# Layer 0 of a two-layer trunk: smaller triangular inverses, one shared tile, and a new order of the steps

## The chip, the cores and the metric

The kernel runs on one core of a Trainium2 chip. The metric is the device time of one launch in microseconds. The kernel before was timed in three runs: median 1544.08 us, from 1541.60 to 1544.83.

## The reference

The program is a two-layer encoder trunk over 1024 tokens of width 1024, in float32, with a conditioning vector that scales, shifts and gates each layer. Layer 0 feeds one input projection into two kinds of bidirectional heads; layer 1 (a 31-tap convolution and dilated attention) is not touched by the change but for the place of its tiles. What matters here is layer 0, cut to its core:

```python
# even layer: four mLSTM heads (dk 64, dv 128) and four gated DeltaNet heads (128, 128)
mq, mk, mv, mo, mg, dqkv, dg, z = split(h @ w_in)
# mLSTM, per chunk, state C:  num = w*(q @ C) + (exp(d - m) * (q k^T)) @ v ;  C = wold*C + kw^T v
out_a = sigmoid(mo) * head_rms(mlstm(forward) + mlstm(backward))
# DeltaNet: qkv = silu(conv5(dqkv)), q and k normalised per head
a    = strict_tril(beta * (k k^T) * gam)
u, w = solve(a + I, beta*v), solve(a + I, beta*exp(gc)*k)     # the triangular inverse
v_new = u - w @ S ;  o = (q*exp(gc)) @ S + (q k^T * gam) @ v_new
S     = exp(gl)*S + (k*exp(gl - gc))^T v_new
out_b = head_rms(gdn(forward) + gdn(backward))
mix   = concat(out_a, out_b) * silu(z) ;  y = mix @ w_out ;  x = x + gate * y
```

The recurrences run over chunks, forward and backward, so a step of either kind needs the state of the step before it in its direction.

## The kernel before, in words

Tokens are cut into eight chunks of 128 (`NCH`). Activations lie transposed, features on partitions. A projection of 128 output columns (`in0`, through `project` and `prod`) splits weights and activations into a high and a low part and sums three products: 2 halves of tokens x 8 blocks of features x 3 = 48 matmuls of 512 columns. `wsplit` loads the weights on SP's queue, ScalarE makes the high part, GpSimd the low part (line 241). Output tiles (`y`, in `out_tile`) are 48 matmuls each as well.

Instructions are written in program order and a scheduler orders each engine's queue by it, with program order as priority; each engine then runs its queue in order and waits on semaphores. Nearly all DMAs of layer 0 go out from SP's one queue, also in order. Weight columns for the modulation (`modulation`, lines 428 to 432) are loaded and summed a piece at a time between projections.

Layer 0 in program order: the first key projections and gates; `dn_scales`; eight `dn_system` calls (per chunk: `KK` = k k^T, decay masks built by ScalarE and GpSimd, products on VectorE at line 637, a transpose `NT`, both stored to DRAM); then a list of steps: DeltaNet queries and values (`dn_q`, `dn_v`: a projection, a five-tap convolution on VectorE at lines 373 to 391, turns by TensorE), mLSTM queries, keys and values (`m_q`, `m_k`, `m_v`), all eight mLSTM steps at once (`mlstm`), `dn_inverse`, and the first gates; then the eight `dn_step` calls, the other gates (`gate_chunk`, `gate_pair`: z and mo projections), and the output tiles (`out0`).

`dn_inverse` holds 128 triangular blocks of 64x64 (2 directions, 2 halves, 8 chunks, 4 heads), one on each partition, as `NL`, and eliminates column by column on VectorE: per column a product into `iv` (line 663) and an addition (line 666), cut in halves where the rectangle passes 512 elements. It then stores the blocks to DRAM (`xl_d`) as they are and transposed. `dn_step` loads its piece as `Y`, joins the two blocks of a chunk with two small products `T` through `aux`, and then computes `kS`, `Yr`, `KQ`, `qS`, `dS` and `o`, for direction 0 (`d=0`) and then direction 1.

PSUM: two banks for projections, and a pool of banks `t`, `A`, `B`, `C` (1, 2, 2, 1) for the rest. SBUF: pools on the right side that are opened and closed as the layer goes on.

## Time and profile before

| what | value |
|---|---|
| median of three runs | 1544.08 us |
| the profiled execution's own time | 1542.68 us |
| its span in the trace | 1540.9 us |
| mean granted clock of TensorE | 0.928 |
| TensorE, VectorE, ScalarE, GpSimd busy | 1338.6, 979.4, 635.4, 605.3 us |
| layer 0, layer 1 | 0 to some 884 us, 884 to 1541 us |

Sums are made against the profiled execution; the 1.8 us between its time and its span are start and end, and it is 1.4 us below the median. In the rows below, PE is TensorE, PEld its weight loads, DVE VectorE, ACT ScalarE, POOL GpSimd, SP the engine that issues DMAs. A row of windows has the stretch, its length, busy time and number of instructions of PE, PEld, DVE, ACT and POOL, then the granted clock as a share of 2.4 GHz, the share of the DMA engines and GB/s. A row of a group has the line, engine, operation, output and inputs, shapes and count, then busy time and mean duration in ns, then idle time before it; matmuls overlap, so a mean is more than the distance from one to the next. A row of one line (`x106: a/b/c`) has the shortest, median and longest duration in ns, then the first and last start.

### The profile page before, as it was taken

To read this page: it belongs to the slowest core of one execution; us is meant where nothing else is said; L and a number is where in the kernel's file an instruction comes from. 1 tells how busy PE (TensorE), PEld (TensorE's weight loads), DVE (VectorE), ACT (ScalarE), POOL (GpSimd) and SP (SyncE) were. 2 spreads that over 40 slices of the span, in tenths; PEclk is the share of its full clock that TensorE was granted. 3 is DMA by queue.
4 is the path that set the end of the run, shared out by engine and by line. 5 is a ranking of instruction groups with operands and counts; after the bars stand their busy time and mean duration, and the time that the engine had idled before them with its cause. 6 is when DMAs were issued, how large, how long until landed. Compare 5 with 4: busy or idle time off the path is not lost.

```text
span 1540.9 us, 20550 instructions
## 1 busy us (share of the span) xinstructions
PE 1338.6 (87%) x7195; PEld 1059.1 (69%) x7195; DVE 979.4 (64%) x1712; ACT 635.4 (41%) x1481; POOL 605.3 (39%) x433
## 2 busy tenths in 40 slices
PE   3978767887877889889999979778999999999998
PEld 2767655666665667778877857556777777777776
DVE  6789346999889442345854427999984445345544
ACT  5354456433444513433453323335335633425322
POOL 3562325563464332110243117998514215122210
PEclk9999987998888999979999999989999899998999
DMA  9333669444654886454736261001123115244332
GB/s 312 94 91 78 130 143 235 129 125 135 184 165 133 276 267 203 117 155 145 224 118 205 83 135 49 28 28 42 42 87 111 48 56 189 73 123 157 120 113 107
DMA packets 235658, 202.50 MB, mean 131 GB/s; under 512 B 38591, under 2 KB 198867, under 8 KB 235427
## 3 DMA queue, kind: packets, MB, share of 16 engines
q1 hardware_dynamic: 214755, 190.70, 42.9%
q10 hardware_dynamic: 20800, 10.49, 2.4%
q8 instruction: 57, 0.93, 0.3%
q14 instruction: 46, 0.38, 0.1%
HBM read 146.87 MB, written 57.93 MB: 133 GB/s over the span
## 4 chain that ended last, share of the span: by engine, by line
PE 35%; DVE 11%; DMA 4%; issue 2%; ACT 2%; POOL 0%; SPq 0%; ACTq 0%; POOLq 0%; DVEq 0%
PE y L121 9%; DVE u L1220 8%; PE z L121 6%; PE sc L121 3%; PE av L121 3%; PE ob L121 2%; PE pT L136 2%; PE aq L121 2%; PE ak L121 2%; DMA z_d<-nb_d 1%; PE gb L121 1%; PE vps L136 1%; DMA g<-mix_d 1%; ACT junk L1040 1%; PE dS L121 0%
## 5 line engine op out<-in xcount | busy, mean ns | idle before, releaser
L241 POOL TENSOR_TENSOR wlo<-wraw,whi 128x1024 fp32r<-128x1024 f32 x60 | 158.2, 2637 | 238.5 <-ACT whi L240 224.8
L1220 DVE SCALAR_TENSOR_TENSOR u<-xp,cw,u 128x1009 f32<-128x1009 f32 (+14 forms) x90 | 174.6, 1941 | 2.1
L1210 POOL TENSOR_TENSOR u<-u,cv 128x512 f32<-128x512 f32 (+15 forms) x60 | 120.5, 2010 | 17.3 <-ACT cv L1209 13.8
L432 POOL TENSOR_TENSOR macc<-macc,ada 128x512 f32<-128x512 f32 x56 | 89.6, 1599 | 76.9 <-ACT ada L430 64.1
L121 PE MATMUL z<-hhi,whi 128*128 128x512 f32 x256 | 106.8, 417 | 1.9 <-ACT mo L719 1.9
L121 PE MATMUL z<-hlo,whi 128*128 128x512 f32 x256 | 105.5, 412 | 0.0
L121 PE MATMUL z<-hhi,wlo 128*128 128x512 f32 x256 | 105.4, 412 | 0.0
L121 PE MATMUL y<-wohi,mhi 128*128 128x512 f32 x240 | 96.4, 403 | 1.4 <-ACT mhi L1010 1.4
L121 PE MATMUL y<-wohi,mlo 128*128 128x512 f32 x240 | 95.4, 399 | 0.6 <-DVE mlo L1011 0.5
L121 PE MATMUL y<-wolo,mhi 128*128 128x512 f32 x240 | 95.9, 399 | 0.0
L240 ACT CAST whi<-wraw 128x1024 fp32r<-128x1024 f32 x60 | 62.6, 1043 | 72.4 <-PE gb L121 15.6
L666 DVE TENSOR_TENSOR NL<-NL,iv 128x440 f32<-128x440 f32 (+40 forms) x106 | 92.1, 897 | 0.5
L663 DVE TENSOR_TENSOR iv<-NL 128x440 f32<-128x440 f32 (+40 forms) x106 | 87.5, 858 | 1.4
L591 POOL TENSOR_SCALAR_AFFINE_SELECT E<-E 128x512 f32<-128x512 f32 x32 | 22.7, 709 | 149.0 <-DMA E<-gc_d 57.6
L430 ACT ACTIVATE ada<-ada,cs 128x512 f32<-128x512 f32 x56 | 40.4, 725 | 80.7 <-DMA ada<-in_ada_w_dram 79.6
L1209 ACT ACTIVATE cv<-xp,cw 128x512 f32<-128x512 f32 (+15 forms) x60 | 42.4, 718 | 55.5 <-POOL u L1210 55.2
L1372 DVE COPY PT<-pT 128x512 f32<-128x512 f32 x48 | 32.4, 688 | 48.2 <-PE pT L136 48.1
L1349 ACT ACTIVATE pt<-pt,o 128x256 f32<-128x256 f32 (+1 forms) x64 | 31.4, 491 | 75.6 <-DVE o L1345 73.2
L121 PEld LDWEIGHTS z<-hhi,whi 128*128 128x128 f32 x256 | 49.7, 194 | 14.9 <-ACT mo L719 2.3
L121 PEld LDWEIGHTS z<-hlo,whi 128*128 128x128 f32 x256 | 49.8, 195 | 11.7 <-issue 1.1
L121 PEld LDWEIGHTS z<-hhi,wlo 128*128 128x128 f32 x256 | 49.8, 195 | 11.6 <-issue 1.0
L1345 DVE CUSTOM_DVE_ANT_0 pt<-sc,bias 128x256 f32<-128x256 f32 (+1 forms) x64 | 25.8, 403 | 48.8 <-PE sc L121 28.8
(449 smaller groups left out, 3718.5 us busy)
## 6 DMA issues: line engine op xcount, KB each, us to landing
wraw<-in_ev_w_in_dram SPq DMA_DIRECT2D x32, 512.0 KB
ada<-in_ada_w_dram SPq DMA_DIRECT2D x64, 256.0 KB
wraw<-in_od_w_in_dram ACTq DMA_DIRECT2D x20, 512.0 KB
x<-in_x_dram SPq DMA_DIRECT2D x16, 512.0 KB
ada<-in_ada_w_dram SPq DMA_DIRECT2D x16, 512.0 KB
od_d<-o SPq DMA_DIRECT2D x64, 66.0 KB
n<-od_d SPq DMA_DIRECT2D x4, 1056.0 KB
E<-nmu_d SPq DMA_DIRECT2D x16, 256.0 KB
```

What stands on the lines that cost most here:

```text
L121: return nc.tensor.matmul(o, lhsT=l, rhs=r, start=s, stop=e, skip_group_check=shared).ins
L136: nc.tensor.transpose(o, i, ident[:k, :k])
L240: nc.scalar.copy(out=hi, in_=raw)
L241: nc.gpsimd.tensor_tensor(out=lo, in0=raw, in1=f(hi), op=ALU.subtract)
L430: nc.scalar.mul(out=t_ if k else acc, in_=t_, mul=cs[:, k:k + 1])
L432: nc.gpsimd.tensor_tensor(out=acc, in0=acc, in1=t_, op=ALU.add)
L663: nc.vector.tensor_tensor(out=t_, in0=NL[:, a_:b_, k:k + 1].to_broadcast([P, b_ - a_, m]), in1=NL[:, k:k + 1, k + 1:64].to_broadcast([P, b ...
L666: nc.vector.tensor_tensor(out=NL[:, a_:b_, k + 1:64], in0=NL[:, a_:b_, k + 1:64], in1=t_, op=ALU.add)
L1209: nc.scalar.mul(out=t_, in_=xp[:, lo + d:hi + d], mul=w_)
L1210: nc.gpsimd.tensor_tensor(out=y[:, lo:hi], in0=y[:, lo:hi], in1=t_, op=ALU.add)
L1220: nc.vector.scalar_tensor_tensor(out=y[:, lo:hi], in0=xp[:, lo + d:hi + d], scalar=w_, in1=y[:, lo:hi], op0=ALU.mult, op1=ALU.add)
L1372: nc.vector.tensor_copy(out=PT, in_=tb)
```

## The change

Five things are changed together.

1. **One tile.** The right-side pools are gone; one tile `U` of 128 x 8448 floats is there for the whole kernel, and `sl` and `ring` cut slices and rotating slices out of it. The six early PSUM banks become the fixed pool `psb` from the start. Some tags get other banks: turns use only bank `t`, T and KQ too; kS, Yr and dS are on `A`, qS and o on `C`; the mLSTM products on `B`. Both directions of `dn_step` draw E from one ring of two, `aux` has one buffer.
2. **The inverse.** VectorE eliminates only the 32x32 diagonal blocks (30 columns, 30 products and 30 additions). The off-diagonal block of each 64x64 block is computed on TensorE as a product of three, in four rounds: `first_product` spreads Z over a block diagonal on VectorE (ZD), iG multiplies it by AT; GD spreads that, iV multiplies by B, iT transposes the result. Z, AT and B are read back from `xl_d` by 12 DMAs, and the results are written back to it by 8.
3. **The order.** The systems and the inverse come after two value projections and the first DeltaNet head; the mLSTM and DeltaNet steps come one by one between the gate projections and, at the end, the output tiles.
4. **mLSTM operands by chunk.** q, k, v and the weighted queries are stored to DRAM (`mqk_d`, `mv_d`, `qt_d`) and loaded per chunk; the weighting is done once over all tokens on GpSimd. DeltaNet queries are loaded per chunk too (`dqc`).
5. The two convolutions that ran on ScalarE and GpSimd (`conv5s`, query head 3 and value head 2) run on VectorE like the others.

```diff
+    U = pool("pu", 1).tile([P, 8448], F32, name="U")
...
+    n_r, nt_r = ring(0, 4, 8, P), ring(4096, 2, 4, P)
...
     def dn_inverse(n):
...
-        for k in range(62, 0, -1):
-            m = 63 - k
-            halves = [(0, k)] if k * m <= 512 else [(0, k // 2), (k // 2, k)]
...
+        D2 = NL.rearrange("p (s x) -> p s x", s=2)[:, :, 0:2048].rearrange("p s (a b) -> p s a b", b=64)[:, :, :, 0:32]
+        for k in range(30, 0, -1):
+            m = 31 - k
+            t_ = iv([2, k, m])
+            nc.vector.tensor_tensor(out=t_, in0=D2[:, :, 0:k, k:k + 1].to_broadcast([P, 2, k, m]),
+                                    in1=D2[:, :, k:k + 1, k + 1:32].to_broadcast([P, 2, k, m]), op=ALU.mult)
+            nc.vector.tensor_tensor(out=D2[:, :, 0:k, k + 1:32], in0=D2[:, :, 0:k, k + 1:32], in1=t_, op=ALU.add)
...
+        for t_, src, j, i in ((Z, xl_d[0], 0, 1), (AT, xl_d[1], 0, 0), (B, xl_d[0], 1, 1)):
+            for d, b, g_ in lanes4:
+                nc.sync.dma_start(out=t_[g_], in_=part(src, d, b, j, i))
...
+        def first_product(r):
+            nc.vector.tensor_tensor(out=ZD, in0=spread(Z[:, 8 * r:8 * r + 8, :]), in1=own, op=ALU.mult)
+            ps = bank(nm("iG"), (P, 8, 32), "A")
+            for u in range(8):
+                mm(ps[:, u, :], ZD[:, u].rearrange("p g i -> p (g i)"), AT[:, 8 * r + u, :], True, True)
+            return ps
+
+        ps = first_product(0)
+        for r in range(4):
+            nc.vector.tensor_tensor(out=GD, in0=spread(ps), in1=own, op=ALU.mult)
+            if r < 3:
+                ps = first_product(r + 1)
+            pv = bank(nm("iV"), (P, 8, 32), "C")
+            for u in range(8):
+                mm(pv[:, u, :], GD[:, u].rearrange("p g i -> p (g i)"), B[:, 8 * r + u, :], True, True)
+            nc.scalar.copy(out=Z[:, 8 * r:8 * r + 8, :], in_=pv)
...
+        for d, b, g_ in lanes4:
+            nc.sync.dma_start(out=part(xl_d[0], d, b, 0, 1), in_=Z[g_])
...
-        (conv5s if h in (3,) else conv5)(xp, h, y)
+        conv5(xp, h, y)
...
-                for q in range(2):
-                    nc.gpsimd.tensor_tensor(out=qt[:, q, :], in0=mq[q][:, tcs], in1=qt[:, q, :], op=ALU.mult)
+                qt = next(qt_r)
+                nc.sync.dma_start(out=qt, in_=qt_d[d, :, :, tcs].rearrange("q p t -> p q t"))
+            v_ = next(mv_r)
+            nc.sync.dma_start(out=v_[:, :, 0:P], in_=mv_d[tcs])
...
-    for step, n in ((dn_q, 0), (dn_v, 0), (m_q, 0), (dn_q, 1), (m_q, 1), (dn_q, 2), (dn_q, 3), (m_k, 1), (m_v, 0), (m_v, 2), (m_v, 3), (m_v, 1), (m_k, 0), (mlstm, 0), (dn_v, 1), (dn_inverse, 0), (gate_chunk, 0), (dn_v, 2), (gate_chunk, 1), (dn_v, 3)):
...
+    dn_scales()
+    for step, n in ((m_v, 0), (m_v, 1), (dn_q, 0), (dn_v, 0), (dn_lanes, 0), (m_v, 2), (m_v, 3), (m_q, 0), (m_q, 1),
+                    (dn_q, 1), (dn_v, 1), (dn_q, 2), (dn_v, 2), (dn_q, 3), (dn_v, 3)):
         step(n)
...
-                    B_ = Bs[d_] = etile(("E", "Em")[d_])
+                    B_ = Bs[d_] = etile("E")
...
-            aux = pc.tile([P, 2, 4, 64], F32, tag="aux", name=nm("aux"))
+            aux = next(aux_r)
...
-    marks = [dn_step(j) for j in range(NCH)]
...
+    for step, n in ((dn_step, 0), (m_k, 0), (m_k, 1), (gate_chunk, 0), (dn_step, 1), (mlstm, 0), (gate_chunk, 1), (dn_step, 2),
+                    (gate_chunk, 2), (mlstm, 1), (dn_step, 3), (gate_chunk, 3), (mlstm, 2), (gate_chunk, 4), (gate_chunk, 5),
+                    (dn_step, 4), (mlstm, 3)):
+        step(n)
...
+    for j, ti, after in ((5, 3, (4,)), (6, 4, (2,)), (7, 2, (1,))):
+        dn_step(j)
+        with tc.issue_after(half_done):
             out0(ti, None, after)
+        mlstm(j)
```

Three places show what moves on TensorE's queue. The first is DeltaNet's systems (`KK` and `NT` of a chunk, `turn` a transpose of something else). Before, the last of the eight chunks stand so:

```order
L136 MATMUL NT_1318<-ident,N_1292 128x128 x4
L136 MATMUL NT_1357<-ident,N_1331 128x128 x4
L121 MATMUL KK_1404<-kT_666 128x128
L121 MATMUL KK_1404<-kT_667 128x128
L121 MATMUL KK_1404<-kT_668 128x128
L121 MATMUL KK_1404<-kT_669 128x128
L121 MATMUL gps_1556<-macc_773,one 1x512
L136 MATMUL turn_1652<-ident,vT_1644 128x128 x4
L136 MATMUL turn_1660<-ident,vT_1644 128x128 x4
L136 MATMUL turn_1539<-ident,qT_1520 128x128 x4
L136 MATMUL NT_1396<-ident,N_1370 128x128 x4
L136 MATMUL NT_1435<-ident,N_1409 128x128
```

After, in the second value projection of those that follow the systems (`mv` is a wide projection matmul):

```order
L139 MATMUL mv_2057<-hlo_41_242,whi_2049 128x512
L139 MATMUL mv_2057<-hhi_37_238,wlo_2050 128x512
L139 MATMUL mv_2057<-hhi_38_239,whi_2049 128x512
L139 MATMUL mv_2057<-hlo_42_243,whi_2049 128x512
L158 MATMUL turn_1153<-ident,vT_1094 128x128 x4
L139 MATMUL KK_1596<-kT_656 128x128
L139 MATMUL KK_1596<-kT_657 128x128
L158 MATMUL NT_1515<-ident,U 128x128 x4
L139 MATMUL KK_1596<-kT_658 128x128
L139 MATMUL KK_1596<-kT_659 128x128
L139 MATMUL KK_1633<-kT_656 128x128
L139 MATMUL KK_1633<-kT_657 128x128
```

The chunks that stood one behind the other now have a run of projection matmuls between them: 21 stand between the KK rows ahead of this piece and these, 25 behind them.

The second place is the start of DeltaNet's steps, whose first product is `T`. Before, it stands within a gate projection (`mo`):

```order
L121 MATMUL mo_5915<-hhi_44_241,wlo_5911 128x512
L121 MATMUL mo_5915<-hhi_45_242,whi_5910 128x512
L121 MATMUL mo_5915<-hlo_49_246,whi_5910 128x512
L121 MATMUL mo_5915<-hhi_45_242,wlo_5911 128x512
L121 MATMUL T_736_4487<-aux_4484 64x64 x4
L121 MATMUL mo_5915<-hhi_45_242,whi_5910 128x512
L121 MATMUL mo_5915<-hlo_49_246,whi_5910 128x512
L121 MATMUL mo_5915<-hhi_45_242,wlo_5911 128x512
```

After, it stands behind the last round of the block products (`iV`, `iT`; `mo_3320` is gate 0):

```order
L139 MATMUL mo_3320<-hhi_46_247,whi_3285 128x512
L139 MATMUL iV_1924<-U 128x32 x8
L139 MATMUL mo_3320<-hlo_50_251,whi_3285 128x512
L139 MATMUL mo_3320<-hhi_46_247,wlo_3286 128x512
L139 MATMUL mo_3320<-hhi_46_247,whi_3285 128x512
L139 MATMUL mo_3320<-hlo_50_251,whi_3285 128x512
L139 MATMUL mo_3320<-hhi_46_247,wlo_3286 128x512
L158 MATMUL iT_1934<-ident,U 128x128 x2
L139 MATMUL T_324_2896<-U 64x64 x4
L139 MATMUL T_325_2902<-U 64x64 x4
L139 MATMUL KQ_2909<-dqc,kT_656 128x128
```

The last iT, whose result goes to DRAM and is read back as Y, is now followed by T and by the products of both directions of the step, with no projection between.

The third place is the middle of DeltaNet's steps. Before, step after step stands without a projection:

```order
L121 MATMUL T_778_4732<-Y_4719,aux_4723 64x64 x4
L121 MATMUL dS_4700<-v_771_4693,ke_4691 128x128 x4
L121 MATMUL o_4709<-vv_4671,E_4650 128x128 x4
L121 MATMUL Yr_4775<-vv_4764,Y_4719 128x128 x4
L121 MATMUL T_792_4819<-aux_4816 64x64 x4
L121 MATMUL kS_4859<-S_4545,kT_666 128x128
L121 MATMUL kS_4859<-S_4545,kT_667 128x128
L121 MATMUL kS_4859<-S_4545,kT_668 128x128
L121 MATMUL kS_4859<-S_4545,kT_669 128x128
```

After, in step 1 (`Cps` and `num` belong to the mLSTM step, `mo` to gate 1):

```order
L139 MATMUL kS_3482<-U,kT_658 128x128
L139 MATMUL kS_3482<-U,kT_659 128x128
L139 MATMUL Cps_3671<-mvc,qtkw 64x129 x4
L139 MATMUL num_3682<-mvc,E_3678 128x129
L139 MATMUL qS_3502<-U,dqc 128x128 x4
L139 MATMUL num_3682<-mvc,E_3678 128x129
L139 MATMUL mo_4108<-hlo_39_240,whi_4103 128x512
L139 MATMUL mo_4108<-hhi_35_236,wlo_4104 128x512
L139 MATMUL mo_4108<-hhi_35_236,whi_4103 128x512
L139 MATMUL T_388_3448<-U 64x64 x4
```

The DeltaNet rows now have mLSTM rows and projection rows between them.

## Rows read from the trace of the kernel before

**Rows 1.** The page's head and part 1: busy time of each engine.
```profile
span 1540.9 us, 20550 instructions
PE 1338.6 (87%) x7195; PEld 1059.1 (69%) x7195; DVE 979.4 (64%) x1712; ACT 635.4 (41%) x1481; POOL 605.3 (39%) x433
```

**Rows 2.** Windows by stage: length, busy (instructions) PE PEld DVE ACT POOL, clock, DMA.
```profile
105.00:205.00 100.00, 81.76 (x360) 65.96 (x361) 69.71 (x84) 45.30 (x132) 36.58 (x35) 0.88 0.43 99
205.00:250.00 45.00, 27.30 (x123) 21.39 (x122) 25.11 (x58) 25.09 (x77) 11.74 (x15) 0.77 0.88 210
250.00:400.00 150.00, 122.70 (x548) 96.49 (x546) 134.26 (x171) 60.75 (x146) 80.91 (x57) 0.91 0.56 143
400.00:525.00 125.00, 100.88 (x457) 76.76 (x457) 93.09 (x155) 57.64 (x119) 59.76 (x49) 0.86 0.58 182
525.00:580.00 55.00, 46.28 (x314) 35.62 (x315) 26.65 (x98) 17.85 (x45) 22.23 (x27) 0.97 0.83 265
580.00:710.00 130.00, 113.47 (x689) 98.37 (x689) 46.26 (x124) 53.07 (x146) 22.20 (x30) 0.86 0.55 150
710.00:790.00 80.00, 77.09 (x533) 65.89 (x532) 59.44 (x147) 36.22 (x107) 21.31 (x18) 1.00 0.61 188
790.00:884.00 94.00, 92.89 (x438) 74.33 (x437) 44.27 (x76) 35.28 (x95) 25.56 (x27) 1.00 0.40 131
884.00:1541.00 657.00, 601.36 (x3404) 465.84 (x3402) 402.84 (x658) 253.12 (x551) 273.90 (x134) 0.95 0.30 89
```

**Rows 3.** Two full stretches, as windows, and the wide groups of the second.
```profile
75.00:100.00 25.00, 25.00 (x109) 20.09 (x108) 19.90 (x17) 16.62 (x22) 19.76 (x17) 1.00 0.42 116
725.00:785.00 60.00, 57.09 (x412) 48.71 (x411) 49.52 (x119) 30.69 (x89) 16.57 (x15) 1.00 0.68 211
...
L121 PE MATMUL z<-hlo,whi 128*128 128x512 f32 x21 | 8.7, 415 | 0.0
L121 PE MATMUL y<-wohi,mhi 128*128 128x512 f32 x5 | 2.1, 416 | 0.8 <-ACT mhi L1010 0.8
```

**Rows 4.** TensorE's waits, 105 to 884 us: us in total, times, longest.
```profile
PE S L121 <- DVE E L773: 10.4, 5, 3.2
PE turn L136 <- DVE kT L379: 8.0, 1, 8.0
PE turn L136 <- DVE modc L196: 8.0, 1, 8.0
PE dq L121 <- POOL wlo L241: 7.7, 1, 7.7
PE KK L121 <- DVE N L637: 6.1, 1, 6.1
```

**Rows 5.** VectorE's inverse and convolution lines by group and form; GpSimd's select.
```profile
L666 DVE TENSOR_TENSOR NL<-NL,iv 128x440 f32<-128x440 f32 (+40 forms) x106 | 92.1, 897 | 0.5
L663 DVE TENSOR_TENSOR iv<-NL 128x440 f32<-128x440 f32 (+40 forms) x106 | 87.5, 858 | 1.4
...
L663 DVE TENSOR_TENSOR iv<-NL 128x510 f32<-128x510 f32 x2 | 1.4, 683 | 0.0
...
L663 DVE TENSOR_TENSOR iv<-NL x106: 225/635/2874, 272.1 to 502.3; 128x440 f32<-128x440 f32 x6, 128x486 f32<-128x486 f32 x4, 128x480 f32<-128x480 f32 x4, 128x468 f32<-128x468 f32 x4
...
L377 DVE SCALAR_TENSOR_TENSOR kT<-xp,cw,kT x16: 1268/1276/3420, 84.5 to 137.3; 128x1024 f32<-128x1024 f32 x16
...
L591 POOL TENSOR_SCALAR_AFFINE_SELECT E<-E 128x512 f32<-128x512 f32 x32 | 22.7, 709 | 149.0 <-DMA E<-gc_d 57.6
```

**Rows 6.** Timeline around the inverse, SP and ACT: start us, length, instruction.
```profile
255.76 2.29 SPq L655 DMA_DIRECT2D NL<-nd_d  x2
...
503.51 0.45 SPq L669 DMA_DIRECT2D xl_d<-NL  x1
...
536.02 0.32 SPq L673 DMA_DIRECT2D xl_d<-iv  x1
...
518.57 1.08 ACT L672 COPY iv<-NL 128x512 f32<-128x512 f32 x1 [7.49 <-DMA xl_d<-iv]
```

333 lines of the change are left out of this document (177 added, 156 removed).

## The prediction

> **What bounds the kernel now.** I read the shares of busy time first, then the program cut into stages, then the waits of TensorE, then VectorE's own rows and the DMA rows around the inverse. TensorE is busy for 1338.6 of 1540.9 us [rows 1], so it is the engine to feed; a gain must come from its idle time, or from time at the lower of its two clock levels (1.2 and 2.4 GHz). The stages show where that is [rows 2]: from 105 to 710 us each stage has both an idle share and a granted clock under 1.00; from 710 to 884 us TensorE is full at clock 1.00; after 884 us comes layer 1, which the change leaves as it is but for where its tiles lie. So the argument is about 105 to 884 us, 779 us.
>
> How much of the 779 us is loss? Two prices at full clock are enough [rows 3]. From 75 to 100 us TensorE runs without a gap: 109 matmuls, 108 of them of 512 columns, in 25.00 us, 0.2315 us each. From 725 to 785 us it does 412 in 57.09 us, of which three groups of 21 z and 14 y (groups of 5, 5 and 4) are wide; 57.09 - 77 x 0.2315 = 39.3 us for 335 small ones, 0.117 us each. The eight stages hold 3462 matmuls [rows 2]; 28 projections and 8 output tiles of 48 make 1728 wide ones, and 1734 are small. Floor: 1728 x 0.2315 + 1734 x 0.117 = 603 us. Loss: 779 - 603 = **176 us**. The same from the stages, idle + (1 - clock) x length: 30, 28, 41, 42, 10, 35, 3, 1, together 190, an upper bound, since a stretch at half speed that is also idle is counted twice; I scale them by 0.93 to 28, 26, 38, 39, 10, 32, 3, 1. The change can win from these and nothing else.
>
> The waits name the causes [rows 4]: a mask product S on VectorE (10.4), a turn on the first convolved key (8.0), a turn on a bank held for the modulation column (8.0), a weight split on GpSimd (7.7), the next system on VectorE's scaling (6.1). Two are VectorE being late while it runs the inverse: L663 and L666 take 179.6 us of it between 272 and 503 us [rows 5].
>
> **The change part by part.**
>
> *Floor.* The inverse gets 64 matmuls of 32 columns and 8 transposes. No row has that shape; at the small price 72 x 0.117 = 8 us, at half or twice that 4 to 17. I take 8, the price of the neighbours.
>
> *Front, until DeltaNet's first systems (was 28).* The first turn still waits for the first convolved key; that wait (8.0) and the slow clock behind it stay, 12 us. The split wait (7.7, with clock 10) may come anywhere a weight is late: kept. What goes is the rest: two value projections (96 wide, 22 us) that need no VectorE now stand there while it catches up on the keys. I take 22, bounds 12 and 28.
>
> *Systems and inverse, until the first block product (was 26 + 38, and part of 39).* Before, the systems stood in a bunch with hardly a projection between; after, one per twenty-odd wide matmuls. That removes the KK wait. But now the in-order queue of TensorE ends at the first block product iG, which needs the inverse's elimination, a write of 4 MB, and a read back. Count from the end of the fourth projection after the change (dv of head 0). TensorE's own work to iG is 11.5 projections (mv 2 and 3, mq 0 and 1, dq and dv 1 to 3, mk 0 and half of mk 1), 128 us, plus some 184 small ones, 21 us: 149. The other path: TensorE to the end of dq 1, 70 us; then VectorE does four convolutions before the elimination is done. One has six operations at about 1.28 us [rows 5], 7.7 us; with the port contention that L377's maximum of 3.42 shows I allow 9.4: 31 to 38, middle 34. Elimination: the smallest operation (62 elements) took 225 ns and one of 510 took 683 [rows 5], so 162 ns + 1.02 ns an element. The old one had 106 per line with 41,664 elements, 60 us a line, 119 for both, where 179.6 was measured: 1.5 times. The new one has 30 per line and 9,920 elements: 15 us a line, 30 undisturbed, 45 at 1.5; middle 38. Two vt products, 3. Then the write: before, from the issue at 503.5 to the last at 536.0 us, 32.5 us, with ScalarE held 7.5 us by its two buffers [rows 6]; there are three now: 20 to 34, middle 27. Then the new read back, 12 DMAs of 32x32x32, 12,288 pieces of 128 bytes. Nearest row: the four loads of NL, 8,192 pieces of 256 bytes, issued at 255.8, first use at 272.1 [rows 5, 6], 16.3 us. By bytes (1.5 of 2 MB) that is 12 us, by pieces 24; middle 18. Sum 70 + 34 + 38 + 3 + 27 + 18 = 190 against 149: TensorE stands **42 us** with rounding; all low ends give 166, a wait of 17; all high ends 213, a wait of 64. Waits before iG cost nothing more, since this path is the longer. I take 42, bounds 15 and 66.
>
> *Block products and first DeltaNet step.* Between iG and the last transpose iT stand about 110 wide matmuls (25 us) in pieces of 12 to 20, so the four rounds are covered. Behind iT the order has T of step 0 at once, no projection between. T needs the write-back (8 DMAs, 8,192 pieces of 128 bytes) and the loads of Y. By bytes 8 us, by pieces 16 (same NL row), plus 4 us for the start and landing of the write and of Y's loads behind it (no row shows a short transfer alone; by bytes 64 KB would be 0.5 us of NL's 16.3, so this is mostly latency, and an estimate): 12 to 20, middle 16. The step's own chain follows with no cover, two directions, about 8 us, and some 5 us of slow clock after it (from 105 to 205 us the clock of 0.88 means 24 us at the lower level, for three such gaps [rows 2]): 29, bounds 18 and 45.
>
> The Trainium skill, DMA: Bandwidth & Descriptors, Specifications, says that transfers under 512 bytes do not reach line rate and are done as read-modify-write. By that rule the write-back would cost up to twice the upper figure, 16 us more in this part; no run here shows a 128-byte write, and my sum doesn't use it.
>
> *DeltaNet and mLSTM steps, gates, output (was the rest of 39, and 10, 32, 3, 1: 85).* Before, all mLSTM steps ran while VectorE was in the inverse, which is the S wait; and the last DeltaNet steps of the bunch had no projections left between them, in the stage that lost 16.5 us idle at a clock of 0.86 [rows 2]. After, every pair of steps has z and mo between its parts, and the last three have y. What stays is a share: one bank for turns and T, one buffer for aux, two E buffers for both directions. I take half, rounded down, 40, bounds 20 (three quarters won) and 85 (nothing won). The mLSTM operands by chunk add DMAs on SP's single queue; DMA share in these stages was 0.40 to 0.83 [rows 2], so bandwidth has room, and I cost it at nothing; if that cover fails it shows in this term.
>
> Two convolutions go from ScalarE and GpSimd to VectorE, some 16 us of it, inside the sum above.
>
> **Sum.** Loss after: 22 + 42 + 29 + 40 = 133. Stretch: 603 + 8 + 133 = 744, against 779: 35 us less. The profiled execution took 1542.7 (span 1540.9), 1.4 under the median of the runs, 1544.08: forecast **1509 us**.
>
> **The rivals.**
>
> *A. Nearly all loss goes.* Elimination undisturbed, transfers at their byte price, chains covered: 12 + 15 + 18 + 20 = 65, floor 607: 672, 107 less, 1437. For it: 710 to 790 us shows DeltaNet steps among projections at clock 1.00 with 77 of 80 us busy [rows 2]. Against: two round trips through DRAM stand on TensorE's queue that weren't there.
>
> *B. The round trips eat it.* With the inverse path at its high end (66 + 45) and the rest as forecast: 22 + 111 + 40 = 173, floor 611: 784, 5 more; with either of them halfway, 10 to 20 less. About 1530 to 1549. For it: a transfer of small pieces, at a price that no row shows, is on the path twice. Against: the NL loads, in pieces of 256 bytes, moved 2 MB in 16.3 us [rows 6]. The rule of the Trainium skill above (DMA: Bandwidth & Descriptors, Specifications) would favour it, since the write-back's 16 us more make 1525.
>
> *C. Slower: the two directions of a DeltaNet step run one after the other.* Before, direction 0 used E and direction 1 Em, two buffers each; now both draw on one ring of two, and a first visit takes both. So in steps 0 to 3 direction 1's decay mask can only be loaded when direction 0's o is done and its partner is stored. Its price per direction: a load of 256 KB, an exp, a select (709 ns on GpSimd) and a product of 512 elements (683 ns) [rows 5], under 6 us with the load, and aux with one buffer adds a load in all eight steps, 3 us: 8 visits of 6 and 16 of 3 are 96 us if bare. Half bare takes back the 45 won in the last part and gives 1557; all bare 1605. It decides when fewer than some 20 wide matmuls (5 us) stand between the directions' parts; the order has 41 between the two KQ of step 1, but none in step 0 and only a few beside the o and dS rows.
>
> **How the numbers follow.** Forecast (15 to 65 us less) 0.45; A 0.18; B 0.15; C 0.22. A measurement of this kernel can tell 0.2%, 3 us, from no change. Faster: 0.45 + 0.18 + 0.11 of B = 0.74; same 0.04 of B; slower 0.22 with C. Low end: half of A lies beyond 1445; high end: a third of C lies beyond 1562. So 1445 to 1562; the forecast's own range is 1479 to 1529.
>
> **What would show it.** TensorE waiting on VectorE's first ZD product (or on the DMA of Z behind it) for 15 to 66 us; T of step 0 waiting 12 to 20 on Y's load; L693 and L695 together 30 to 45 us; S and KK gone from the top of the waits; clock near 1.00 once projections stand between the steps. Wrong would be: TensorE's idle between steps 1 and 7 above 50 us with E or aux as the releaser (C); no wait at iG (A); or a layer 1 that differs from 657 us by more than 5.

## The result: slower, and the profile after

The changed kernel took 1605.69 us (median of four runs, 1600.88 to 1609.30), the kernel before on the same chip 1542.84 (four runs). The ratio is **1.0417, 95% interval 1.0391 to 1.0442**: 63 us slower, where the forecast was 35 us faster. The time lies outside the range and on the other side of no change. The kernel before differs between chips (medians 1543 to 1556 us beside the experiments below), so kernels of different calls are compared by their ratio alone.

The page of the kernel after, head and part 1 (against [rows 1]):

```profile
span 1599.1 us, 20599 instructions
PE 1366.1 (85%) x7331; PEld 1087.1 (68%) x7331; DVE 873.7 (55%) x1565; ACT 630.8 (39%) x1479; POOL 576.8 (36%) x390
```

VectorE got 106 us lighter, as intended, and the program 58 us longer in its span. TensorE has 136 more instruction records (7331 against 7195).

The first matmul of layer 1 (`gb`) tells where the time went: it starts at 945.3 us after and 884.1 before. Tile rows (shortest, median and longest duration in ns, first and last start) give it, first that of the kernel before, then those of the kernel after, with the block products and the mLSTM products `num`:

```profile
L121 PE MATMUL gb<-hhi,whi x64: 387/396/774, 884.1 to 996.2; 128*128 128x512 f32 x64
...
L139 PE MATMUL gb<-hhi,whi x64: 387/397/776, 945.3 to 1062.0; 128*128 128x512 f32 x64
...
L139 PE MATMUL iG<-U x64: 191/276/401, 387.8 to 414.4; 128*128 128x32 f32 x64
...
L139 PE MATMUL num<-mvc,E x128: 272/275/583, 532.1 to 829.4; 128*128 128x129 f32 x128
```

Layer 0 lost 61 us; layer 1 took 653.8 us against 656.8. The windows of the kernel after, by stage (columns as in [rows 2]):

```profile
105.00:200.00 95.00, 79.27 (x373) 64.68 (x374) 70.82 (x97) 52.80 (x160) 41.57 (x32) 0.91 0.47 117
200.00:240.00 40.00, 29.39 (x126) 22.55 (x125) 10.64 (x34) 17.09 (x42) 12.17 (x14) 0.83 0.80 194
240.00:290.00 50.00, 48.17 (x220) 37.98 (x218) 21.14 (x18) 17.65 (x39) 27.68 (x18) 1.00 1.07 274
290.00:388.00 98.00, 69.58 (x282) 54.49 (x283) 84.08 (x92) 46.27 (x99) 45.38 (x32) 0.79 0.63 174
388.00:438.00 50.00, 48.59 (x272) 42.02 (x271) 12.71 (x12) 14.27 (x25) 18.99 (x10) 0.93 0.44 130
438.00:451.00 13.00, 0.15 (x2) 0.07 (x2) 0.00 (x0) 1.03 (x2) 2.89 (x3) 0.63 0.94 172
451.00:500.00 49.00, 37.66 (x205) 31.98 (x206) 14.11 (x27) 15.52 (x46) 4.37 (x8) 0.82 0.65 172
500.00:580.00 80.00, 69.95 (x384) 55.46 (x383) 26.40 (x65) 38.71 (x97) 29.86 (x26) 0.89 0.73 209
580.00:660.00 80.00, 68.03 (x407) 56.65 (x406) 26.45 (x69) 35.83 (x104) 18.50 (x22) 0.93 0.65 177
660.00:722.00 62.00, 60.05 (x353) 48.84 (x352) 33.49 (x82) 22.26 (x48) 10.03 (x6) 0.95 0.67 215
722.00:773.00 51.00, 30.68 (x144) 23.98 (x143) 21.37 (x72) 11.96 (x40) 6.52 (x4) 0.59 0.71 216
...
860.00:945.00 85.00, 70.59 (x307) 54.22 (x305) 32.69 (x60) 25.40 (x70) 17.85 (x17) 0.87 0.23 78
```

I price each stretch as the prediction did (its wide matmuls by 0.2315 us, its small ones by 0.117; what is over is loss). By the trace's own counts the 779 us of before hold a floor of 607 and a loss of 172, the 840 us of after a floor of 622 and a loss of 218:

| stretch after | loss, us | what it is |
|---|---|---|
| 105 to 200 | 21 | front |
| 200 to 388 | 59 | systems, convolutions, elimination |
| 388 to 438 | 4 | the four rounds of block products |
| 438 to 451 | 13 | T of step 0 waits |
| 451 to 500 | 18 | the bare step behind it (no projection beside it) |
| 500 to 722 | 40 | DeltaNet and mLSTM steps among gate projections |
| 722 to 773 | 34 | mLSTM and DeltaNet with no projection |
| 773 to 945 | 29 | last steps and output tiles |

Before, the stretch from 781 us to layer 1, where the output tiles stand, lost 4 us. In after's 722 to 773 the granted clock is 0.59, near the lower of the two levels (0.50 is 1.2 GHz), behind gaps of several us. TensorE's waits, 105 to 945 us (against [rows 4]; in us the total, the times, the longest):

```profile
PE Cps L139 <- issue: 18.8, 3, 8.5
PE T L139 <- DMA U<-xl_d: 14.2, 2, 12.8
PE dv L139 <- ACT xp L394: 10.5, 2, 5.9
PE o L139 <- ACT U L1024: 9.7, 4, 5.9
PE turn L158 <- DVE modc L220: 9.0, 2, 6.6
PE turn L158 <- DVE kT L403: 8.6, 1, 8.6
```

The first is an mLSTM product; `issue` is time in which the engine waited for nothing that the profile shows. The chain of work that ended last, 727 to 773 us of the kernel after (start, length, what), shows how these gaps lie:

```profile
727.13 7.73 issue
734.87 1.13 PE Cps L139 x8
736.00 4.64 PE num L139 x16
740.64 8.46 issue
749.10 1.13 PE Cps L139 x8
750.23 4.64 PE num L139 x16
754.88 2.51 issue
757.39 1.13 PE Cps L139 x8
...
772.88 2.00 PE y L139 x4
```

Three half steps of mLSTM (one direction of a step each) go by one at a time, 8 to 14 us each, 5.8 of it TensorE's work, and only then can the first output tile start: it needs the mix of tile 3, which needs mLSTM step 4, and step 4 stands behind the last gate projection, whose last z starts at 721.2. The output weights are not what it waits for: their last part is split by 737 us.

### The profile page after: what moved, and what is told of

Same layout as the page of the kernel before. It is cut to its first block, busy times and chain, and to the rows that moved or that the text cites. A ratio compares the mean times of both kernels' runs of the same rounds, so it can differ in the third digit from the quotient of the medians.

```text
span 1599.1 us, 20599 instructions
## 1 busy us (share of the span) xinstructions
PE 1366.1 (85%) x7331; PEld 1087.1 (68%) x7331; DVE 873.7 (55%) x1565; ACT 630.8 (39%) x1479; POOL 576.8 (36%) x390
## 4 chain that ended last, share of the span: by engine, by line
PE 46%; DVE 14%; DMA 11%; issue 8%; ACT 4%; POOL 3%; SPq 2%; POOLq 0%; ACTq 0%; DVEq 0%
PE y L139 11%; DVE u L1294 7%; PE z L139 6%; PE sc L139 3%; PE av L139 3%; DMA E<-nmu_d 2%; PE ob L139 2%; PE aq L139 2%; PE num L139 2%; PE pT L158 2%; DMA U<-in_ada_w_dram 2%; DMA E<-gc_d 2%; PE mo L139 2%; PE ak L139 2%; PE T L139 1%
## 5 line engine op out<-in xcount | busy, mean ns | idle before, releaser
L1294 DVE SCALAR_TENSOR_TENSOR u<-xp,U,u 128x1009 f32<-128x1009 f32 (+14 forms) x90 | 174.9, 1945 | 2.1
L455 POOL TENSOR_TENSOR U<-U 128x512 f32<-128x512 f32 x56 | 84.4, 1507 | 75.0 <-ACT U L453 64.9
L139 PE MATMUL y<-wohi,mhi 128*128 128x512 f32 x240 | 100.1, 417 | 3.9 <-ACT mhi L1087 3.9
L453 ACT ACTIVATE U<-U,cs 128x512 f32<-128x512 f32 x64 | 45.6, 721 | 99.2 <-DMA U<-in_ada_w_dram 92.4
L1283 ACT ACTIVATE cv<-xp,U 128x512 f32<-128x512 f32 (+15 forms) x60 | 42.3, 718 | 54.7 <-POOL u L1284 54.5
L139 PEld LDWEIGHTS y<-wohi,mhi 128*128 128x128 f32 x240 | 47.4, 198 | 16.5 <-ACT mhi L1087 5.5
L1446 DVE COPY U<-pT 128x512 f32<-128x512 f32 x48 | 32.3, 687 | 45.8 <-PE pT L158 45.6
L139 PEld LDWEIGHTS y<-wohi,mlo 128*128 128x128 f32 x240 | 46.6, 195 | 12.0 <-DVE mlo L1088 1.1
L139 PEld LDWEIGHTS y<-wolo,mhi 128*128 128x128 f32 x240 | 47.3, 197 | 10.7
```

The source lines that it names most:

```text
L139: return nc.tensor.matmul(o, lhsT=l, rhs=r, start=s, stop=e, skip_group_check=shared).ins
L453: nc.scalar.mul(out=t_ if k else acc, in_=t_, mul=cs[:, k:k + 1])
L455: nc.gpsimd.tensor_tensor(out=acc, in0=acc, in1=t_, op=ALU.add)
L1283: nc.scalar.mul(out=t_, in_=xp[:, lo + d:hi + d], mul=w_)
L1294: nc.vector.scalar_tensor_tensor(out=y[:, lo:hi], in0=xp[:, lo + d:hi + d], scalar=w_, in1=y[:, lo:hi], op0=ALU.mult, op1=ALU.add)
L1446: nc.vector.tensor_copy(out=PT, in_=tb)
```

## Experiments: the shared buffers

My first theory was that the rings and banks of the change are the price: in those half steps `om` has one buffer, stored to DRAM and reloaded (in the second of the gaps above SP issues the reload at 743.38 and VectorE can use it from 748.14), and the mix of an output tile draws `om` and `n` from the ring of three (`h`) that layer 1's transposes use too. Rival C of the prediction held the shared E ring of DeltaNet's directions guilty.

**Run x1_mix_tiles**, the mix's tiles back on the E rings as in the kernel before (`om` of the early mixes drew on `h` there too):

```diff
-        om = htile("om").rearrange("p (h d) -> p h d", h=4)
+        om = htile("om").rearrange("p (h d) -> p h d", h=4) if early else etile("E")
...
-            n_ = htile("n").rearrange("p (h d) -> p h d", h=4)
+            n_ = etile("Em")
```

> The changed kernel with one thing undone: in mix0 the tiles om and n of the output tiles come from E and Em again (two buffers each) and not from the three shared half tiles. Theory 1, buffers: the stretch from 840 to 945 us of the changed kernel lost 26 us against its own matmuls, because the next tile's om can't be loaded while the last one's n is in use; 12 to 22 us come back, some 1588 us. Theory 2, order: the last steps of both recurrences now come after most of the output tiles, so their end is late whatever buffer they use; under 5 us come back, 1601 to 1606 us.

Measured: 1631.73 us against 1555.60 before, ratio 1.0508 [1.0459, 1.0557], slower than the change itself. TensorE's waits of this run from 600 to 960 us have a new head: the mix's product on GpSimd, now written to an E tile, comes late, on a ring that DeltaNet's and mLSTM's steps use too.

```profile
PE nT L158 <- POOL E L1128: 34.5, 4, 14.2
```

**Run x2_om_cps**, a second `om` buffer from mLSTM step 4 on, and `Cps` on another bank:

```diff
-            om = next(om_r)
+            om = next(om_r if j < 4 else om2_r)
...
-                ps = bank(nm("Cps"), (P, 2, P + 1), "B")
+                ps = bank(nm("Cps"), (P, 2, P + 1), "C")
```

> The changed kernel with two things freed on the mLSTM chain: a second om buffer from step 4 on, and Cps on bank C and not on B beside the two num banks. Theory 1, buffers: from 722 to 773 us four half steps of mLSTM stand bare at 8 to 14 us each, since Cps waits for a bank that num holds until om has gone to DRAM and the next has come back; 15 to 28 us of the 34 lost there come back, some 1584 us. Theory 2, order: the bare stretch is as long as the output weights need to load and be split, and what fills it makes no difference; under 5 us.

Measured: 1626.28 us, ratio 1.0457 [1.0429, 1.0485]; the interval overlaps that of the changed kernel, so neither a gain nor a loss is shown. The bare half steps did get shorter (6 to 7.4 us), and the first output tile still came at 772.7 (before this edit 772.8). But the last gate projection ends 6 us later in this run (its last z starts at 727.3), so the bare stretch shrank from 51 to 45 us, and its loss from 34 to some 30. The tile row of the output tiles:

```profile
L139 PE MATMUL y<-wohi,mhi x240: 389/397/796, 772.7 to 1613.6; 128*128 128x512 f32 x120
```

The head of TensorE's waits in this run, 600 to 960 us:

```profile
PE nT L158 <- POOL n L1129: 16.7, 4, 6.8
```

So single buffer and bank are not what most of the 34 us hang on: with the half steps shorter the stretch still waits, in part on the mix (5.0 of these 16.7 us fall before the first output tile).

**Run x3_e_tags**, the E ring by direction, as before:

```diff
-                B_ = etile("E")
+                B_ = etile(("E", "Em")[d])
```

> The changed kernel with the decay tiles of a DeltaNet step as before: E for direction 0 and Em for direction 1, where Em is also the mLSTM's. Rival C of the prediction: the ring of two that both directions share is what made the steps slow, so 15 to 40 us come back. Theory 1: the shared E costs little, since the queue has matmuls between the directions, and Em is now shared with the mLSTM; between 8 us faster and 8 us slower.

Measured: 1643.55 us, ratio 1.0567 [1.0538, 1.0596]. Rival C's ring, undone, gives nothing back. In this order Em is the mLSTM's ring too, so this run alone doesn't clear the shared ring; the waits on E shown with the rivals below do.

## Experiments: the inverse alone, the order alone

**Run b1_inverse_alone**: the kernel before, with 32x32 elimination, block products and both trips, and nothing else of the change (the code is that of the change, on a tile `NL_` of the old pools):

```diff
-    NL = pb.tile([P, 64, 64], F32, name="NL")
+    NL_ = pb.tile([P, 5184], F32, name="NL", bufs=1)
...
-        for k in range(62, 0, -1):
+        for k in range(30, 0, -1):
```

> The kernel before with the new inverse alone (32x32 elimination, block products on TensorE, two trips through DRAM), its order, pools and operands as before; VT lies in a page and the transposing copies have two buffers, for want of room. Theory 1: the new inverse is no loss in itself. It takes 135 us from VectorE between 272 and 503 us, where TensorE lost 76 us, adds 17 us of matmul records to TensorE, and its trips are covered by the gates and values that stand around it: 5 to 25 us faster, some 1530 us. Theory 3: the two trips are what made the changed kernel slow; then 10 to 30 us slower, 1555 to 1575 us.

Measured: 1612.13 us, ratio 1.0375 [1.0331, 1.0420], slower than either theory had it. Windows of this run:

```profile
275.00:335.00 60.00, 51.22 (x227) 41.07 (x227) 55.07 (x70) 26.91 (x67) 37.70 (x21) 0.91 0.44 130
...
400.00:525.00 125.00, 51.87 (x360) 41.79 (x362) 31.35 (x142) 27.59 (x82) 26.80 (x42) 0.66 0.62 178
```

The elimination is over before 335 us, and then TensorE is busy for 52 of 125 us at a clock of 0.66, where before it was 101 of 125 at 0.86 [rows 2]. All eight mLSTM steps stand there with hardly a projection between (23 wide matmuls from 400 to 560 us; loss 102). Before, 400 to 503 us held 215 wide matmuls, with a loss of 37. So it is not the inverse's own work that is slow there; with it alone the queue comes out with the recurrence bare.

**Run p1_old_inverse**: the changed kernel, with the old 64x64 elimination and without block products and their trips:

```diff
-        for k in range(30, 0, -1):
-            m = 31 - k
+        for k in range(62, 0, -1):
+            m = 63 - k
...
-        ps = first_product(0)
```

> The changed kernel with the old elimination of 64x64 blocks on VectorE and without the block products and their two trips through DRAM. The elimination now stands among six convolutions, so VectorE has 130 us more to do on the path to the first DeltaNet step, of which the trips and rounds (some 45 us) come off: 40 to 90 us slower than the changed kernel, a ratio of 1.07 to 1.10. If the trips were what made the change slow, it would be no slower than the changed kernel, 1.04 or less.

Measured: 1657.09 us against 1547.30, ratio 1.0696 [1.0661, 1.0732], at the low end of what was expected: in the new order the new inverse is worth 2.8 points (hundredths of the ratio), some 43 us. In this run VectorE's elimination is back (groups of VectorE, 200 to 600 us):

```profile
L697 DVE TENSOR_TENSOR U<-U 128x440 f32<-128x440 f32 (+40 forms) x106 | 77.8, 765 | 0.5
L694 DVE TENSOR_TENSOR U<-U 128x440 f32<-128x440 f32 (+40 forms) x106 | 69.6, 690 | 2.0 <-DMA U<-nt_d 0.5
```

**Run o2_order_before**: everything of the changed kernel in before's order of steps:

```diff
+    for ch in range(NCH):
+        dn_system(ch)
...
+    for j in range(NCH):
+        mlstm(j)
...
+    marks = [dn_step(j) for j in range(NCH)]
+    for cidx in range(2, 6):
+        gate_chunk(cidx)
```

> The changed kernel with the order of the kernel before: systems in a bunch, all mLSTM steps in a run, the inverse late, then all DeltaNet steps; the new inverse, the one tile, the banks and the operands from DRAM are kept. If the new order were what made it slow, this would return to 1.00 to 1.01. If inverse, banks and operands made it slow, and the new order hides part of that, it is slower still: a stretch of 416 small matmuls without a projection on TensorE's queue, at some 10 us a half step of mLSTM, gives 1.05 to 1.10. I expect the second.

Measured: 1723.74 us, ratio 1.1134 [1.1094, 1.1175], slower than expected. From 600 to 850 us hardly a projection is left (18 wide matmuls), in the windows of this run:

```profile
600.00:850.00 250.00, 152.94 (x822) 136.25 (x823) 62.45 (x166) 46.89 (x150) 11.71 (x24) 0.62 0.46 111
```

What of tile, banks and operands from DRAM makes this so much worse than b1 (1.0375) in the same order is not separated. The heads of its TensorE waits from 400 to 1000 us are iG on the read back (19.5 us, one wait) and T, 17.0 us with nothing shown and 16.9 us on a mask product E.

**Run o1_mlstm_early**: the changed kernel with one list altered, into which the calls of mLSTM steps 4 to 7 that stood behind it move too. mLSTM starts before DeltaNet, and its last step stands ahead of the last pair of gate projections in the list.

```diff
-    for step, n in ((dn_step, 0), (m_k, 0), (m_k, 1), (gate_chunk, 0), (dn_step, 1), (mlstm, 0), (gate_chunk, 1), (dn_step, 2),
-                    (gate_chunk, 2), (mlstm, 1), (dn_step, 3), (gate_chunk, 3), (mlstm, 2), (gate_chunk, 4), (gate_chunk, 5),
-                    (dn_step, 4), (mlstm, 3)):
+    for step, n in ((m_k, 0), (m_k, 1), (mlstm, 0), (gate_chunk, 0), (mlstm, 1), (dn_step, 0), (gate_chunk, 1), (mlstm, 2), (dn_step, 1),
+                    (gate_chunk, 2), (mlstm, 3), (mlstm, 4), (dn_step, 2), (gate_chunk, 3), (mlstm, 5), (dn_step, 3), (gate_chunk, 4),
+                    (mlstm, 6), (gate_chunk, 5), (mlstm, 7), (dn_step, 4)):
...
-    mlstm(4)
...
-        mlstm(j)
```

> The changed kernel with only the list of steps altered: both mLSTM keys first, and all eight mLSTM steps between the gates, so that the last of them is behind before the output weights load; the DeltaNet steps as they were, a place later. Theory 2, order: the bare mLSTM steps from 722 to 773 us (34 us lost) and the late end of the output tiles (26 us lost) come from recurrence steps that were left over when the projections ran out; 30 to 60 us come back, a ratio of 0.995 to 1.02 to the kernel before. Theory 1, buffers: the steps cost as much wherever they stand; a ratio of 1.035 to 1.05.

Measured: 1576.67 us, ratio 1.0181 [1.0151, 1.0211]: 2.4 of the 4.2 points come back, some 36 us. Tile rows of this run:

```profile
L139 PE MATMUL gb<-hhi,whi x64: 387/397/774, 917.9 to 1035.8; 128*128 128x512 f32 x64
...
L139 PE MATMUL y<-wohi,mhi x240: 389/397/796, 750.6 to 1571.4; 128*128 128x512 f32 x120
```

The first output tile starts 22 us earlier and layer 1 27 us earlier than after, with every buffer, bank and DMA as the change has them. A bare rest is left: the last z starts at 728.9, and mLSTM runs to 747 us.

**Run b2_inverse_spread**: b1 with its mLSTM steps one by one between projections (`mlstm` called per step):

```diff
+                    (mlstm, 0), (dn_q, 2), (mlstm, 1), (dn_q, 3), (mlstm, 2), (dn_v, 1), (dn_inverse, 0), (mlstm, 3), (dn_v, 2), (mlstm, 4), (dn_v, 3),
+                    (mlstm, 5), (gate_chunk, 0), (mlstm, 6), (gate_chunk, 1), (mlstm, 7)):
```

> The kernel before with the new inverse, as in the run with the inverse alone, but the mLSTM steps put one by one between the projections that follow. That run lost 100 us between 400 and 560 us, where all mLSTM steps stood on TensorE's queue without a projection and the inverse behind them. Theory 2, order: with a projection beside each step 40 to 80 us of it come back, a ratio of 0.985 to 1.01. Theory 3, trips: the inverse's two trips cost it, wherever the steps stand; 1.03 to 1.04.

Measured: 1589.50 us, ratio 1.0254 [1.0213, 1.0295], against 1.0375 for b1 and between the two theories: in the kernel before, too, the new inverse gains from the spread (loss 400 to 560: 59 instead of 102), and still doesn't pay.

## Experiments: the front, the block products, the last load

**Runs q1, q2 and q3**, on o1. q1 puts a DeltaNet convolution between any two mLSTM projections behind the first DeltaNet head, q2 is q1 with `om` of the mixes (tiles 0, 5, 6, 7) from the ring Em, q3 is q1 with two convolutions back on ScalarE and GpSimd (the first pair of lines below is q1, the next q2, the last q3).

```diff
-    for step, n in ((m_v, 0), (m_v, 1), (dn_q, 0), (dn_v, 0), (dn_lanes, 0), (m_v, 2), (m_v, 3), (m_q, 0), (m_q, 1),
-                    (dn_q, 1), (dn_v, 1), (dn_q, 2), (dn_v, 2), (dn_q, 3), (dn_v, 3)):
+    for step, n in ((m_v, 0), (m_v, 1), (dn_q, 0), (dn_v, 0), (dn_lanes, 0), (dn_q, 1), (m_v, 2), (dn_v, 1), (m_v, 3),
+                    (dn_q, 2), (m_q, 0), (dn_v, 2), (m_q, 1), (dn_q, 3), (dn_v, 3)):
...
-        om = htile("om").rearrange("p (h d) -> p h d", h=4)
+        om = htile("om").rearrange("p (h d) -> p h d", h=4) if early else etile("Em")
...
-        conv5(xp, h, y)
+        (conv5s if h in (3,) else conv5)(xp, h, y)
```

> The run with the mLSTM steps early, and in the first list the convolved projections (dq, dv) put alternately with the plain ones (mv, mq) in place of behind them. In the changed kernel VectorE was idle for most of 205 to 280 us and then busy for 84 of 98 us, while TensorE lost 40 us from 290 to 388 us. Theory 2, order: VectorE starts on the convolutions some 50 us earlier and TensorE no longer waits for them; 15 to 30 us less than the run with the mLSTM steps early, a ratio of 0.998 to 1.01 to the kernel before. Theory 3, trips: iG waits for the elimination and its trips, which come no earlier; under 8 us.

> As the run with the convolutions spread, and om of the output tiles from the Em ring, which the mLSTM steps have left by then, so that the three half tiles serve n alone. Theory 1, buffers: the last 100 us before layer 1 lost 27 us in the run with the mLSTM steps early, and 8 to 20 us of it come back. Theory 2, order: the end waits for the last DeltaNet step and its mix, whatever the buffer; under 5 us, or a loss where the ring is still in use.

> As the run with the convolutions spread, and query 3 and value 2 convolved on ScalarE and GpSimd again, as in the kernel before. If VectorE is still what TensorE waits for ahead of the block products, 5 to 15 us less than that run; if the elimination's trips are, between 5 us faster and 5 us slower, since they start no earlier.

Measured: 1.0178 [1.0123, 1.0233], 1.0171 [1.0122, 1.0221] and 1.0183 [1.0136, 1.0230]. None differs from o1. In q1 the loss of 290 to 388 us falls from 42 to 25, and that of 240 to 290 rises from 2 to 12 and of 388 to 438 from 5 to 10: the waits move.

**Run r1_no_products**: o1 without iG, iV, iT, ZD and GD, so without the off-diagonal part of the inverse; both trips stay.

```diff
-            for u in range(8):
-                mm(ps[:, u, :], ZD[:, u].rearrange("p g i -> p (g i)"), AT[:, 8 * r + u, :], True, True)
...
+        nc.scalar.copy(out=VT.rearrange("p g c j -> p c g j"), in_=Z.rearrange("p (c g) j -> p c g j", g=4))
```

> The order of run o1 with the block products left out: no iG, iV or iT on TensorE, no ZD and GD on VectorE, the blocks are read from DRAM and written back unmultiplied (so the off-diagonal part of the inverse is not computed, and the output differs). Both trips through DRAM and every bank, ring and order stay. Theory (the 28 us by which o1 stays above before are for some 17 us the 136 records of the products, the rest a scatter of short waits): ratio about 1.007 (1.004 to 1.010), layer 1 begins 15 to 20 us earlier than in o1, near 900. Rival 1 (the products are filled into gaps and cost nothing): ratio 1.016 to 1.020 as o1. Rival 2 (the products also stretch the chain from the elimination to T of step 0, and the steps behind it): ratio 1.000 or below, layer 1 near 885.

Measured: 1555.70 us against 1551.62, ratio 1.0027 [1.0000, 1.0053]. The block products cost o1 1.5 points, some 24 us: more than their records' price (16), not quite the second rival's. T of step 0, their successor, starts at 450.7 us instead of 477.1.

**Run t1_last_mix** and **t2_after_last_mix**. The kernels with the shared tile lose about 20 us in the last stretch of layer 0, where before lost 4 (o1 from 860: 18; r1: 18; the changed kernel 22). SP's rows of the kernel after, 860 to 925 us (start, length, line, DMA), say why:

```profile
899.86 0.32 SPq L1160 DMA_DIRECT2D x_d<-U  x1
912.66 0.32 SPq L1173 DMA_DIRECT2D U<-x_d  x1
913.15 0.32 SPq L1114 DMA_DIRECT2D om<-oml_d  x1
```

`om` of the last tile goes out at 913.15, directly behind a reload of x that SP holds until the transposes of layer 1's first half (`hps`, the last at 911.93) free its slot; `om` itself draws on the `h` ring, which those same transposes use. Behind it stand squares, a power, two products, eight transposes and the split, and TensorE has 8 us of work from 912 to 932. In the kernel before `om` came from the E ring (`E<-oml_d`, last at 822.49). The edit is for tile 7 alone, when DeltaNet has left the E rings: t1 on o1's list, t2 on the changed kernel.

```diff
-        om = htile("om").rearrange("p (h d) -> p h d", h=4)
+        om = etile("E") if ti == 7 else htile("om").rearrange("p (h d) -> p h d", h=4)
...
-            n_ = htile("n").rearrange("p (h d) -> p h d", h=4)
+            n_ = etile("Em") if ti == 7 else htile("n").rearrange("p (h d) -> p h d", h=4)
```

> The list of o1, and for output tile 7 alone om and n come from the rings E and Em instead of the ring of three that the transposes of layer 1 use too, so that om of the last tile no longer stands behind the reload of x on SP's queue. Theory (the late om is the tail's loss): om of tile 7 is loaded before 850 us instead of at 886, the loss of the last 60 us of layer 0 falls from 18 to 5 or below, layer 1 begins 10 to 15 us earlier, ratio 1.009 to 1.012. Rival (the x reload and the transposes themselves are the wait, om is only beside it): the loss stays at 15 or more, ratio 1.016 to 1.020. Second rival (as in the other runs with a freed buffer, the order elsewhere shifts and gives it back): tail 5, but ratio still above 1.015.

> The changed kernel with the same edit for output tile 7 alone. Theory: the late om costs the changed kernel 10 to 15 us as well, ratio 1.032 to 1.036 against 1.0417 of the changed kernel; om of tile 7 loaded before 875 instead of at 913. Rival (it is beside another wait, or given back elsewhere): ratio 1.039 to 1.045.

Measured: t1 1555.79 us against 1549.51, **1.0040 [1.0006, 1.0073]**; t2 1598.07, 1.0325 [1.0274, 1.0377], where the theory had 1.009 to 1.012 and 1.032 to 1.036: t1 did better than its theory. SP's rows of t1:

```profile
814.46 0.32 SPq L1114 DMA_DIRECT2D E<-oml_d  x1
...
881.78 0.34 SPq L1173 DMA_DIRECT2D U<-x_d  x1
```

And its tile row of layer 1's first product:

```profile
L139 PE MATMUL gb<-hhi,whi x64: 387/394/792, 895.6 to 1010.5; 128*128 128x512 f32 x64
```

`om` now leaves 72 us earlier than in o1, layer 1 starts 22 us earlier, and the loss from 860 us to layer 1 is under 1 us instead of 18. In t2 the same edit is worth 0.9 points, and that loss is 8 us instead of 22. The edit moves `om` and `n` together; which of them counts, and whether it is the ring or the place on SP's queue, is not separated.

**Run t3_no_products_last_mix**: r1 with the edit of t1.

> The run without the block products (r1: the off-diagonal part of the inverse is not computed, so the output differs) with the same edit for output tile 7. Theory (order, products and the late om are three separate prices that add up): ratio 0.993 to 0.997, faster than before. Rival (the prices overlap): ratio 1.000 to 1.004, as r1.

Measured: 1542.15 us, ratio 0.9965 [0.9942, 0.9988], in the theory's band, but the sum is not clean: the late load is worth 1.4 points on o1 and 0.6 on r1, the products 1.5 with it and 0.75 without it. Part of the two prices is one wait.

**Run u1_q3_last_mix**: q3 with the edit of t1.

> q3 (the list of o1, the DeltaNet convolutions spread between the mLSTM projections, two of them back on ScalarE and GpSimd) with the edit of t1 for output tile 7. Theory (the late load hid the gain of the spread convolutions): ratio 0.995 to 1.001, layer 1 begins before 890 us. Rival (the spread only moves the waits, as in q1 to q3): ratio 1.002 to 1.007, as t1.

Measured: 1567.20 us against 1549.29, ratio 1.0105 [1.0086, 1.0124]. Neither: better than q3, worse than t1. Moving the convolutions costs 0.65 points once the end is mended; the late load had hidden no gain of theirs. No kernel that computes the whole reference was faster than before; t1 is the nearest.

## Why the prediction was wrong, point by point

**The step that failed** is "DeltaNet and mLSTM steps, gates, output". It was sized 40 us (half of 85) with bounds 20 and 85. It measured 103: 40 from 500 to 722, 34 from 722 to 773, 29 from 773 to 945. I reasoned that every pair of steps has z and mo between its parts "and the last three have y". I never counted the queue's supply: six gate chunks and the last pair stand beside the first five DeltaNet steps and four mLSTM steps, and no y can run before mLSTM step 4. So four mLSTM steps are left when the gate projections are used up, and the output tiles wait for the first of them. o1 shows it: with one list altered and everything else kept, 36 us come back. [Rows 3] could have said it: z and y both stood among the small matmuls of before at clock 1.00, because in that order all mLSTM steps come ahead of the gates.

Within the same step, the load of the mix operand was not priced at all. t2 gives 0.9 points (14 us) for it in the changed kernel. In the prediction I wrote of the mLSTM operands' added DMAs "bandwidth has room, and I cost it at nothing". `om` of an output tile is not even one of those: the kernel before loads it too, from another ring, and the move of the mix's tiles to the ring `h` stands nowhere in the prediction. It was not bandwidth but the ring behind one DMA, or its place in SP's queue.

Mending both doesn't bring the forecast. In t1 the stretch from 105 us to layer 1 holds a loss of some 170 us by the same prices, where before held 172, and the floor is 16 higher for the block products. So of the 43 us less loss that I forecast (176 to 133) nothing shows in t1.

**Systems and inverse**: 42 forecast, 59 measured (inside the bounds 15 to 66), but not as told. TensorE did not wait at iG (the trace has no idle time before it). The round trip was quicker than I took it: elimination over at 355.6 us, read back issued at 372.98, first iG at 387.8, 32 us where the two DMA terms had 45. The price of the read back also rested on a row that I misread: I took the 16.3 us from NL's first load to its first use as the price of the loads, but in the kernel before VectorE's operation just ahead of that use waits for another product, to 271.46 us, so the 16.3 us are only an upper bound:

```profile
271.46 0.68 DVE L445 TENSOR_TENSOR grow<-gps,grow 1x512 f32<-1x512 f32 x1 [8.08 <-PE gps L121]
```

VectorE's elimination took 22.1 + 25.3 = 47 us (middle 38, bounds 30 to 45), in the groups of the kernel after, 270 to 400 us:

```profile
L695 DVE TENSOR_TENSOR U<-U 128x60 f32<-128x60 f32 (+14 forms) x30 | 25.3, 842 | 0.7
L693 DVE TENSOR_TENSOR U<-U 128x60 f32<-128x60 f32 (+14 forms) x30 | 22.1, 736 | 0.7
```

What TensorE paid was paid earlier: from 290 to 388 us VectorE is busy 84 of 98, projections wait for the page that its convolution still reads (`dv <- ACT xp`, 10.5), and turns for a bank that is free only when VectorE, among its eliminations, has made a modulation column from it (`turn <- DVE modc`, 9.0); the rest is shorter waits and the granted clock of 0.79. I had written that waits before iG cost nothing more since the other path is longer. It was the other way round.

**Block products and first step**: 29 forecast, 4 + 13 + 18 = 35 measured, inside its bounds. T waited 12.8 us, against 16, for a load from `xl_d` (the first T reads `aux`, whose load goes out at 446.29, behind Y's).

```profile
372.98 12.42 SPq L711 DMA_DIRECT2D U<-xl_d  x12
...
437.12 2.82 SPq L738 DMA_DIRECT2D xl_d<-U  x4
440.04 3.66 SPq L740 DMA_DIRECT2D xl_d<-U  x4
443.79 1.68 SPq L980 DMA_DIRECT2D U<-xl_d  x2
...
446.29 0.58 SPq L982 DMA_DIRECT2D U<-xl_d  x1
```

These are SP's rows of the kernel after: the read back, the two write-backs, Y's loads and that of `aux`. From the first write-back's issue at 437.12 to T at 450.9 are 13.8 us. The Trainium skill, DMA: Bandwidth & Descriptors, Specifications, says that transfers under 512 bytes are done as read-modify-write, from which I had estimated up to 16 us more. The trace shows 13.8 us where I had 16 without it, so no such surcharge can be seen here.

**Floor**: 8 us forecast, 15 measured. The price was about right (the first 16 iG records, from 387.77 us to the next product at 389.48, take 0.107 us each, beside wide matmuls 0.235 apart), the count wrong: each float32 product of the 64 stands twice in the records (iG x64 above for 32 products), so 72 instructions are 136 records, 16 us at 0.117. The floor of before was 607 by count, not 603, another 4 us. r1 and t3 put the products' whole price at 0.75 to 1.5 points, 12 to 24 us.

**Front**: 22 forecast, 21 measured; the turn on the first convolved key is still there (8.6, before 8.0 [rows 4]).

Sum of what was off: -1 (front) + 17 + 6 + 63 + 11 (floor) = 96, which is what layer 1's start shows (945.3 us, forecast 884 - 35 = 849). Layer 1 gave 3 back; the profiled execution lies 5 us under the median.

**The other signs.** S no longer waits for VectorE's mask product (10.4 before), but 9.2 us in all for its operands' load and for what the profile doesn't show. KK still waits for VectorE, 6.8 us against 6.1, so the systems' new place removed nothing there. The clock between the steps is 0.89 to 0.95 from 500 to 722 us, and layer 1 differs by 3 us, as I had allowed.

**The rivals.** A and B are out by their numbers. The sign that I gave for A, no wait at iG, did come, without A's gain: it doesn't tell a covered inverse from one that was paid for earlier. C's number for "all bare" was 1605, and the result is 1606, but that is chance: undoing its ring (x3) made the kernel slower, the single `aux` was undone in no run, and E and `aux` (the T copies of line 987) hold TensorE for little in the changed kernel's waits from 451 to 773 us:

```profile
PE T L139 <- ACT U L987: 4.1, 3, 2.1
...
PE o L139 <- DVE E L1007: 2.3, 1, 2.3
```

What C got right is the kind of thing that decided: recurrence steps left without projections beside them. The marker I gave for C (the runs of wide matmuls between a step's parts) looked at the start of the list, where it held; the end of the list was empty.

**Still open.** Why freeing one ring in the changed order costs 0.9 (x1) and 1.5 points (x3); each shifts the scheduler's whole queue, and I did not separate that from the buffer. And what of tile, banks and DRAM operands makes o2 worse than b1.

## What to carry to other kernels

Before a recurrence is spread over an in-order queue, count the supply: how many projections are left when each step is issued, and which step the first later consumer needs; the steps left at the end run bare, 8 to 14 us a half step here, at a granted clock of 0.59. An edit that frees the busiest helper engine is worth what the queue behind it can use: the same inverse was worth 43 us in one order and made the kernel before 57 us slower (b1). And when an operand is moved to another ring, look who else draws on it and what stands ahead of its load on the DMA queue: taking the last output tile's operands off the shared ring, one of them a load of 256 KB behind a reload, gave 10 to 22 us.
